# Two heads per group of score matmuls in a differential attention, and split operands over 128 partitions for a sparse attention's scores

## Chip, cores and metric

One core of a Trainium2 chip runs the whole program, one launch. The metric is the device time of that core in microseconds (us), the median of several executions; a profile of one execution goes with it.

## What is computed

Two blocks on 256 tokens of width 1024, all in float32. The first has two layers; each normalises, projects, and merges three branches (a differential attention, a Hyena convolution, a gMLP). The second has a sparse attention and a block attention side by side, a feed-forward part and a gated embedding. The two places of the change, cut to what matters:

```python
def diff_attend(q, k, v, lam):              # 4 heads, each with two halves m of 64 dims
    s = jnp.einsum('bhmqd,bhmkd->bhmqk', qi, k).astype(jnp.float32) * scale
    p = jax.nn.softmax(s, axis=-1)
    w = p[:, :, 0] - lam * p[:, :, 1]
    return jnp.einsum('bhqk,bhkd->bhqd', w.astype(v.dtype), v)

def nsa_mixer(...):                         # 8 query heads, 2 groups g of keys, 64 dims
    ...
    s = jnp.einsum('bgrcd,bgcmd->bgrcm', qc, kg) * ATTN_SCALE     # selected blocks
    ...
    s = jnp.einsum('bgrqd,bgkd->bgrqk', qb, kb) * ATTN_SCALE      # window
    o = g[..., 0:1] * o_c + g[..., 1:2] * o_s + g[..., 2:3] * o_w
```

In layer 0 the first block's attention works on the tokens and on a context of 256 more; in layer 1 only the tokens ask. At 256 tokens the selected and the window branch of the sparse attention both see all earlier keys.

## The kernel before

**Weights and products.** float32 accuracy is kept by splitting operands: a value is written as hi + lo in float32r (hi is a rounded copy, lo the rest), and a product is three matmuls, hi·hi, hi·lo and lo·hi. Weights are streamed: `unit` (L70 to L84) loads 512 KB with a DMA on SP's queue into `raw` (3 buffers), ACT casts it to `hi` (L81), DVE subtracts to `lo` (L82), four buffers each. The projections (`gemm_a`, `gemm_b`, tiles `hTh` and `hTl` of the activations) accumulate in four PSUM banks, `pg`. Everything else shares the other four, `pm`, taken with `bank()`.

**Order.** A scheduler lays out the instructions of each engine before the run, by its own estimates, and mixes attention matmuls among those of the projections. Matmuls issued with `chain` (`mm`, L60 to L63) keep their program order among themselves, but others may be put between. Each engine, SP's DMA queue too, then executes its own list in order and waits where an operand or a buffer is not ready.

**Differential attention** (`diff_tile`, L579 to L630). For a tile of 128 queries, six tiles over the two layers, four heads in turn: two banks of `pm`, one for each half m; six matmuls (three products, two halves), where the halves m = 0 and 1 lie on partitions 0 to 63 and 64 to 127, so each matmul uses 64 rows of the array; maximum (L599), exponential on ACT (L603), the difference of the two softmaxes, transposes into the first bank (L614), their copy `wT` (L616), the product with v into the second (L61 through `mm`), and the copy `ya` (L622) that frees it. That is 6 x 4 x 6 = 144 score matmuls, 512 keys wide in four of the tiles and 256 in two.

**Sparse attention** (`block2`). `qs[t]` of 128 tokens each are normalised and rotated, then transposed by `trans4` and copied by ACT to `q2T` (L245; L1078, L1079), with group g on partitions 64g to 64g + 63. `ck` is copied out of PSUM and `compress` (L958 on) brings it into the tile `cXF` by four DMAs on SP (L964, L965), adds positions on DVE (L970), and runs 16 float32 compress matmuls each for keys and values against `cw` (two records each). The KV projection follows; its keys are transposed (L1105) and copied by ACT into `kv` (`k2T`, L1106). The scores (L1114 to L1117, `soft_pair` L919 to L927) are one float32 matmul of 64 rows for each of the 8 heads and 2 tiles t, 256 columns wide at t = 0 and 512 at t = 1. float32 operands take two passes of the array here, and the trace has two records for each.

```python
            for i, j in ((0, 0), (0, 1), (1, 0)):
                for m in range(2):
                    r = slice(64 * m, 64 * m + 64)
                    self.mm(sb[m][:, :KN], qT[i][r, h, qt * 128:qt * 128 + 128], kT[j][r, h, k0:k0 + KN],
                            i + j == 0, i == 1, i + j + m > 0)
```

`slabs` (L1282) is a pool of ten buffers of 8 KB per partition, used among others for the modulation weights (`ada`).

Of the kernel before, what the change touches and what calls it, by code (L numbers as in the profile page):

```python
# [7 lines left out]
F32 = mybir.dt.float32  # L8
F32R = mybir.dt.float32r
# [22 lines left out]
class Body:  # L32
# [548 lines left out]
    def diff_tile(self, qt, kT, v, keys, qT, nl, y):  # L581
        nc = self.nc
        k0, KN = keys
        nk = KN // 128
        rs = self.col(4, f"rs{qt}")
        so = self.col(4, "so")
        y = y.rearrange("p (h d) -> p h d", h=4)
        for h in range(4):
            sb = [self.bank(), self.bank()]
            mx = self.col(2, "mx")  # L590
            ss = self.col(2, "ssum")
            p = self.att.tile([128, 2, 512], F32, name=self.nm("p"), tag="p")
            for i, j in ((0, 0), (0, 1), (1, 0)):
                for m in range(2):
                    r = slice(64 * m, 64 * m + 64)
                    self.mm(sb[m][:, :KN], qT[i][r, h, qt * 128:qt * 128 + 128], kT[j][r, h, k0:k0 + KN],
                            i + j == 0, i == 1, i + j + m > 0)
            for m in range(2):
                nc.vector.tensor_reduce(mx[:, m:m + 1], sb[m][:, :KN], axis=AX.X, op=OP.max)  # L599
            nb = self.col(2, "nb")  # L600
            nc.vector.tensor_scalar(nb, mx, -0.125, None, op0=OP.mult)
            for m in range(2):
                nc.scalar.activation(p[:, m, :KN], sb[m][:, :KN], AF.Exp, bias=nb[:, m:m + 1], scale=0.125,  # L603
                                     accum_out=ss[:, m:m + 1])
            r1 = self.col(2, "r1")
            nc.vector.reciprocal(r1, ss)
            cf = self.col(1, "cf")
            nc.vector.tensor_scalar(cf, ss[:, 0:1], r1[:, 1:2], nl, op0=OP.mult, op1=OP.mult)
            nc.vector.tensor_copy(rs[:, h:h + 1], r1[:, 0:1])
            w = p[:, 0, :KN]  # L610
            nc.vector.scalar_tensor_tensor(w, p[:, 1, :KN], cf, w, op0=OP.mult, op1=OP.add)
            tp = sb[0].rearrange("p (k t) -> p k t", k=4)
            for k in range(nk):
                nc.tensor.transpose(tp[:, k], w[:, k * 128:k * 128 + 128], self.ident)  # L614
            wT = self.att.tile([128, 4, 128], F32, name=self.nm("wT"), tag="wT")
            nc.scalar.copy(wT[:, :nk], tp[:, :nk])  # L616
            o = sb[1][:, :128]
            for k in range(nk):
                self.mm(o, wT[:, k], v[:, k0 // 128 + k, h * 128:h * 128 + 128], k == 0, k == nk - 1)
            jk = self.att.tile([128, 128], F32, name=self.nm("aj"), tag="aj")  # L620
            nc.scalar.activation(jk, o, AF.Square, accum_out=so[:, h:h + 1])
            nc.vector.tensor_copy(y[:, h], o)  # L622
        nc.vector.tensor_tensor(so, so, rs, op=OP.mult)
        nc.vector.tensor_tensor(so, so, rs, op=OP.mult)
        r = self.col(4, f"ro{qt}")
        nc.vector.tensor_scalar(so, so, 1.0 / 128.0, EPS, op0=OP.mult, op1=OP.add)
        self.rpow(r, so)
        return r, rs
# [287 lines left out]
            nc.vector.tensor_tensor(tm[:, 1, :, o], d[:, :, i], s, op=OP.mult)  # L916
        nc.vector.tensor_tensor(d[:, :, 0:16], tm[:, 0], tm[:, 1], op=OP.add)

    def soft_pair(self, t, units, fold):  # L919
        banks = [self.bank().rearrange("p (m k) -> p m k", m=2) for _ in units]  # L920
        first = True
        for step in zip(*[mms for mms, _, _ in units]):
            for s, (dst, l, r) in zip(banks, step):
                self.mm(s[:, dst, :128 * (t + 1)], l, r, chain=not first)
                first = False
        for s, (_, vs, hs) in zip(banks, units):
            yield hs, *self.soft_unit(t, s, vs, fold, hs)  # L927

# [109 lines left out]
    def block2(self, x, hTp):  # L1038
        nc, a = self.nc, self.a
# [22 lines left out]
        qT, _ = self.pair("q2T")  # L1062
        for jh in range(2):
            nc.sync.dma_start(w1s[0][jh], a["c_w1"][0, jh])
        qs = [self.tf("w") for t in range(2)]
        kv = self.flat("kv2")
        folds = kv[:, 1536:1632].rearrange("p (i a h) -> p i a h", i=4, a=3)
        fold, mfold = [folds[:, t] for t in range(2)], [folds[:, 2 + t] for t in range(2)]
# [6 lines left out]
        for f in range(2):  # L1075
            for i in range(4):
                self.part_a(us[i], 2 * i, f, op, 256, b[:, f * 256:f * 256 + 256], i == 0, i == 3)
        for t in range(2):  # L1078
            self.trans4(qs[t], qT[:, :, t * 128:t * 128 + 128], None)  # L1079
        ck = self.tf("w")  # L1080
        nc.vector.tensor_copy(ck, b)
        gb = self.gbank()
# [5 lines left out]
        for t in range(2):  # L1088
            tp = self.bank()[:, :24]
            nc.tensor.transpose(tp, gT[:, t * 128:t * 128 + 128], self.ident[:24, :24])  # L1090
            g = self.pcv(24)
# [1 line left out]
            gates.append(g)  # L1093
        self.compress(ck.rearrange("p (v t) -> p v t", v=2), kv[:, 1024:1536].rearrange("p (h d) -> p h d", h=8), w1s)
        bs = self.gemm_b(w[W2CH["KV"]], op, [0, 1])
        k2T = kv[:, :512].rearrange("p (s t) -> p s t", s=2)
        v2 = kv[:, 512:1024].rearrange("p (t s d) -> p t s d", t=2, s=2)
        for t in range(2):
            kn = self.tf("w")[:, :256]
            v4 = bs[t].rearrange("p (s v d) -> p s v d", s=2, v=2)  # L1100
            self.norm_rope(kn, v4[:, :, 0], self.gains[:, 2:4], t, 4)
            nc.vector.tensor_copy(v2[:, t], v4[:, :, 1])
            tp = self.bank()[:, :256].rearrange("p (s t) -> p s t", s=2)
            for s in range(2):
                nc.tensor.transpose(tp[:, s], kn[:, s * 128:s * 128 + 128], self.ident)  # L1105
            nc.scalar.copy(k2T[:, :, t * 128:t * 128 + 128], tp)  # L1106
        ynr = self.flat("ynr")[:, :1024].rearrange("p (t d) -> p t d", t=2)
        for t in range(2):
            y = ynr[:, t].rearrange("p (h d) -> p h d", h=8)
            gt = gates[t][:, 8:24].rearrange("p (m h) -> p h m", m=2)  # L1110
            for i in range(4):
                units = []
                for g in range(2):
                    r = slice(64 * g, 64 * g + 64)  # L1114
                    units.append(([(slice(0, 2), qT[r, i, t * 128:t * 128 + 128], k2T[r, :, :128 * (t + 1)])],
                                  lambda m, k, g=g: v2[:, k, m, 64 * g:64 * g + 64], (2 * i + g, 2 * i + g)))
                for (h, _), o, rs in self.soft_pair(t, units, fold[t]):  # L1117
                    cf = self.col(2, "ucf")
                    nc.vector.tensor_tensor(cf, rs, gt[:, h], op=OP.mult)
                    nc.vector.tensor_scalar(y[:, h], o[:, 0], cf[:, 0:1], None, op0=OP.mult)  # L1120
                    nc.vector.scalar_tensor_tensor(y[:, h], o[:, 1], cf[:, 1:2], y[:, h], op0=OP.mult, op1=OP.add)
# [29 lines left out]
        for t in range(2):  # L1151
            c = slice(t * 128, t * 128 + 128)
            self.trans4(ynr[:, t], ynh[:, :, c], ynl[:, :, c])
        ys = self.scr.tile([128, 1024], F32, name=self.nm("ay"), tag="ay", bufs=1).rearrange("p (t d) -> p t d", t=2)
        for t in range(2):
            KN = 128 * (t + 1)
            y = ys[:, t].rearrange("p (h d) -> p h d", h=8)
            for i0 in (0, 2):
                units = []
                for m in range(2):  # L1160
                    r = slice(64 * m, 64 * m + 64)
# [110 lines left out]
    def run(self):  # L1272
# [6 lines left out]
        self.att = P("att", 2)  # L1279
        self.hT = P("hT", 1)  # L1280
        self.wraw, self.whi, self.wlo = P("wraw", 3), P("whi", 4), P("wlo", 4)
        self.slabs = P("slabs", 10)  # L1282
        self.psg, self.psm = P("psg", 4, True), P("psm", 4, True)
        self.ones = self.const.tile([128, 128], F32, name="ones")
        nc.vector.memset(self.ones, 1.0)
# [167 lines left out]
```

## Time and profile before

| | before |
|---|---|
| median of 3 runs | 1395.8 us (1393.54 to 1398.58) |
| profiled execution | 1392.87 us, span 1390.9 |
| TensorE (PE) busy | 1355.7 us, 97% |
| weight loads (PEld) busy | 1134.1 us, 82% |
| VectorE (DVE) / ScalarE (ACT) busy | 64% / 45% |
| chain that ended last | PE 83%, DVE 7%, DMA 4%, ACT 3% |
| read from memory | 203.37 MB, 147 GB/s over the span |

The span is what the profile covers; the device time is some 2 us more. Busy shares are over the whole span. The chain is followed back from the last instruction, at each step to what released it. PE rows of a timeline give the start and the modelled length of matmuls that overlap, so what one costs is read from start to start of neighbours.

### The profile page before, as it was taken

Reading aid. Unit: us, or ns where it says so; the run is one execution under the profiler, and the core shown is the slowest. Engines: PE = TensorE matmul, PEld = TensorE weight load, DVE = VectorE, ACT = ScalarE, POOL = GpSimd, SP = SyncE. Lnnn points to the kernel's source line nnn. Section 1 sums busy time; section 2 is a strip of 40 time slices with the busy share of each in tenths; the row PEclk is TensorE's granted clock in tenths of the full one; section 3 lists DMA queues with packets and bytes.
Section 4 is the critical chain, followed back from the end, with each engine's and each line's share of the span. In section 5 each row is a group of like instructions: output and inputs, shape, how many; then the busy total and the mean of one; then the engine's idle time right before and its main releaser. Section 6 shows DMA issues by size and latency. Waiting matters only on the chain.

```text
span 1390.9 us, 19805 instructions
## 1 busy us (share of the span) xinstructions
PE 1355.7 (97%) x7721; PEld 1134.1 (82%) x7721; DVE 897.1 (64%) x1574; ACT 621.5 (45%) x1046; POOL 43.3 (3%) x55
## 2 busy tenths in 40 slices
PE   6999999999999999999999999999999999999998
PEld 3786888777888888788688899987878897899996
DVE  3757842685388977388856755667776567655545
ACT  3532432564332334375535644554554645444433
POOL 0000000000000000010000000001002000000000
PEclk9999999999999999999999999999999999999999
DMA  9431222112535545327334255558315356665551
GB/s 388 143 107 61 81 89 92 63 46 67 201 111 191 220 178 183 136 92 234 107 96 135 93 171 187 182 165 289 122 57 160 103 173 193 207 204 191 184 182 46
DMA packets 55261, 206.22 MB, mean 148 GB/s; under 512 B 7102, under 2 KB 8320, under 8 KB 51584
## 3 DMA queue, kind: packets, MB, share of 16 engines
q1 hardware_dynamic: 55168, 204.95, 43.6%
q8 instruction: 61, 1.00, 0.3%
q14 instruction: 32, 0.26, 0.1%
HBM read 203.37 MB, written 1.05 MB: 147 GB/s over the span
## 4 chain that ended last, share of the span: by engine, by line
PE 83%; DVE 7%; DMA 4%; ACT 3%; issue 2%; POOL 1%; SPq 0%; POOLq 0%; ACTq 0%; DVEq 0%
PE pg L61 67%; PE pm L61 13%; DVE lo L82 1%; DMA ada<-ada_w 1%; PE pm L243 1%; DMA f<-hy_f_w 1%; DMA raw<-w_in 1%; ACT hi L81 1%; PE pm L614 1%; DMA xs<-x 1%; ACT p L603 1%; PE pm L947 1%; DVE hTl L67 1%; POOL rstd L145 0%; DVE mx L599 0%
## 5 line engine op out<-in xcount | busy, mean ns | idle before, releaser
L82 DVE TENSOR_TENSOR lo<-raw,hi 128x1024 fp32r<-128x1024 f32 (+1 forms) x242 | 293.6, 1215 | 246.2 <-ACT hi L81 245.1
L81 ACT CAST hi<-raw 128x1024 fp32r<-128x1024 f32 (+1 forms) x242 | 252.1, 1044 | 385.4 <-PE pg L61 332.5
L61 PE MATMUL pg<-hTh,hi 128*128 128x256 f32 (+1 forms) x920 | 305.0, 333 | 1.8 <-DMA f<-hy_f_w 1.4
L61 PE MATMUL pg<-hTl,hi 128*128 128x256 f32 (+1 forms) x920 | 305.2, 332 | 1.1 <-DVE hTl L67 1.1
L61 PE MATMUL pg<-hTh,lo 128*128 128x256 f32 (+1 forms) x920 | 303.9, 331 | 0.3 <-DVE lo L82 0.3
L61 PEld LDWEIGHTS pg<-hTh,hi 128*128 128x128 f32 x920 | 174.0, 189 | 24.5 <-issue 4.2
L61 PEld LDWEIGHTS pg<-hTl,hi 128*128 128x128 f32 x920 | 174.2, 189 | 21.0 <-issue 4.3
L61 PEld LDWEIGHTS pg<-hTh,lo 128*128 128x128 f32 x920 | 174.1, 189 | 18.5 <-issue 2.8
L61 PE MATMUL pg<-lo,hTh 128*128 128x512 f32 x400 | 158.7, 397 | 0.5 <-DVE lo L82 0.5
L61 PE MATMUL pg<-hi,hTh 128*128 128x512 f32 x400 | 158.9, 397 | 0.3 <-ACT hTh L66 0.2
L61 PE MATMUL pg<-hi,hTl 128*128 128x512 f32 x400 | 157.5, 394 | 1.0 <-DVE hTl L67 1.0
L82 DVE TENSOR_TENSOR wsl<-raw,wsl 128x1024 fp32r<-128x1024 f32 x66 | 80.2, 1223 | 70.1 <-ACT wsl L81 69.4
L61 PE MATMUL pg<-hTh,wsl 128*128 128x256 f32 x576 | 105.2, 284 | 0.0
L81 ACT CAST wsl<-raw 128x1024 fp32r<-128x1024 f32 x66 | 68.4, 1048 | 80.3 <-PE pg L61 50.3
L61 PEld LDWEIGHTS pg<-hTh,wsl 128*128 128x128 f32 x576 | 90.5, 192 | 0.3
L61 PEld LDWEIGHTS pg<-hi,hTl 128*128 128x128 f32 x400 | 75.2, 188 | 18.1 <-DVE hTl L67 1.9
L61 PEld LDWEIGHTS pg<-lo,hTh 128*128 128x128 f32 x400 | 75.3, 188 | 17.8 <-issue 2.5
L61 PEld LDWEIGHTS pg<-hi,hTh 128*128 128x128 f32 x400 | 75.2, 188 | 17.4 <-issue 1.5
L61 PE MATMUL pg<-hTl,wsl 128*128 128x256 f32 x288 | 81.7, 284 | 0.0
L61 PE MATMUL pg<-gh,lo 128*128 128x512 f32 (+1 forms) x192 | 64.8, 337 | 0.0
L61 PE MATMUL pg<-gh,hi 128*128 128x512 f32 (+1 forms) x192 | 64.7, 337 | 0.0
L61 PE MATMUL pg<-gl,hi 128*128 128x512 f32 (+1 forms) x192 | 64.6, 337 | 0.0
(363 smaller groups left out, 2031.8 us busy)
## 6 DMA issues: line engine op xcount, KB each, us to landing
raw<-w_in SPq DMA_DIRECT2D x172, 512.0 KB, 3.6
raw<-w_ffn_in SPq DMA_DIRECT2D x36, 512.0 KB, 3.6
ada<-ada_wT SPq DMA_DIRECT2D x16, 1024.0 KB, 6.8
raw<-w_branch SPq DMA_DIRECT2D x24, 512.0 KB, 3.5
raw<-w_out SPq DMA_DIRECT2D x24, 512.0 KB, 3.6
raw<-w_ffn_out SPq DMA_DIRECT2D x22, 512.0 KB, 4.0
ada<-ada_w SPq DMA_DIRECT2D x8, 1024.0 KB, 16.3
cw<-c_w SPq DMA_DIRECT2D x4, 1024.0 KB, 8.6
```

The source lines that it names most:

```text
L61: ins = self.nc.tensor.matmul(out, l, r, start=start, stop=stop)
L67: self.nc.vector.tensor_tensor(lo, src, hi.bitcast(F32), op=OP.subtract)
L81: nc.scalar.copy(hi, raw)
L82: nc.vector.tensor_tensor(lo, raw, hi.bitcast(F32), op=OP.subtract)
L243: nc.tensor.transpose(ps[:, k], src[:, k * 128:k * 128 + 128], self.ident)
L603: nc.scalar.activation(p[:, m, :KN], sb[m][:, :KN], AF.Exp, bias=nb[:, m:m + 1], scale=0.125, accum_out=ss[:, m:m + 1])
L614: nc.tensor.transpose(tp[:, k], w[:, k * 128:k * 128 + 128], self.ident)
L947: nc.tensor.transpose(tp[:, m, k], p[:, m, k * 128:k * 128 + 128], self.ident)
```

## The change

Three edits.

1. `diff_tile`: for each even head all four `pm` banks are taken, and the score matmuls of this head and the next are issued as one chain of twelve, in each product head 1 before head 0 and m = 1 before m = 0. All that follows for a head is as before.
2. `block2`: the queries `qT` are split into hi and lo (a tile `q2s`), and four DMAs for each t, from SBUF to SBUF on SP's queue, bring them to `sq`: hi on partitions 0 to 63 and lo on 64 to 127, for each group g. The keys are split out of PSUM (`k2s`, instead of the copy on ACT), and eight DMAs for each t bring them to `sk`: `a_` = 0 holds hi on both halves of the partitions, `a_` = 1 holds lo on both. A score is then two float32r matmuls over all 128 partitions, accumulated: (q hi, q lo) against hi, and against lo. `soft_pair` accumulates a unit's matmuls with `acc`.
3. `slabs` has 12 buffers; the memory comes from a smaller scratch for dynamic DMAs.

```diff
         for h in range(4):
-            sb = [self.bank(), self.bank()]
+            if h % 2 == 0:
+                sbs = [[self.bank(), self.bank()] for _ in range(2)]
+                go = False
+                for i, j in ((0, 0), (0, 1), (1, 0)):
+                    for hh in (1, 0):
+                        for m in (1, 0):
+                            r = slice(64 * m, 64 * m + 64)
+                            self.mm(sbs[hh][m][:, :KN], qT[i][r, h + hh, qt * 128:qt * 128 + 128],
+                                    kT[j][r, h + hh, k0:k0 + KN], i + j == 0, i == 1, go)
+                            go = True
+            sb = sbs[h % 2]
...
-            for i, j in ((0, 0), (0, 1), (1, 0)):
-                for m in range(2):
-                    r = slice(64 * m, 64 * m + 64)
-                    self.mm(sb[m][:, :KN], qT[i][r, h, qt * 128:qt * 128 + 128], kT[j][r, h, k0:k0 + KN],
-                            i + j == 0, i == 1, i + j + m > 0)
...
-    def soft_pair(self, t, units, fold):
+    def soft_pair(self, t, units, fold, acc=False):
...
+        if acc:
+            for s, (mms, _, _) in zip(banks, units):
+                for i, (dst, l, r) in enumerate(mms):
+                    self.mm(s[:, dst, :128 * (t + 1)], l, r, i == 0, i == len(mms) - 1)
...
+        sq = self.flat("sq", F32R).rearrange("p (g i t) -> p g i t", g=2, i=4)
+        sk = self.flat("sk", F32R).rearrange("p (a g s t) -> p a g s t", a=2, g=2, s=2)
         for t in range(2):
-            self.trans4(qs[t], qT[:, :, t * 128:t * 128 + 128], None)
+            c = slice(t * 128, t * 128 + 128)
+            self.trans4(qs[t], qT[:, :, c], None)
+            hl = self.att.tile([128, 2, 4, 128], F32R, name=self.nm("q2s"), tag="p")
+            self.split(hl[:, 0], hl[:, 1], qT[:, :, c])
+            for g in range(2):
+                for j in range(2):
+                    nc.sync.dma_start(sq[64 * j:64 * j + 64, g, :, c].bitcast(F32), hl[64 * g:64 * g + 64, j].bitcast(F32))
...
-            nc.scalar.copy(k2T[:, :, t * 128:t * 128 + 128], tp)
+            hl = self.att.tile([128, 2, 2, 128], F32R, name=self.nm("k2s"), tag="p")
+            self.split(hl[:, 0], hl[:, 1], tp)
+            for g in range(2):
+                for j in range(2):
+                    for a_ in range(2):
+                        nc.sync.dma_start(sk[64 * j:64 * j + 64, a_, g, :, t * 128:t * 128 + 128].bitcast(F32),
+                                          hl[64 * g:64 * g + 64, a_].bitcast(F32))
...
-                    r = slice(64 * g, 64 * g + 64)
-                    units.append(([(slice(0, 2), qT[r, i, t * 128:t * 128 + 128], k2T[r, :, :128 * (t + 1)])],
+                    q = sq[:, g, i, t * 128:t * 128 + 128]
+                    units.append(([(slice(0, 2), q, sk[:, a_, g, :, :128 * (t + 1)]) for a_ in range(2)],
...
-        self.slabs = P("slabs", 10)
+        self.slabs = P("slabs", 12)
...
-    nc = bacc.Bacc("TRN2", target_bir_lowering=False, num_devices=1)
+    nc = bacc.Bacc("TRN2", target_bir_lowering=False, num_devices=1, dynamic_dma_scratch_size=128)
```

The scheduler lays out the new program, so the order of instructions moves as well. TensorE at the second pair of heads of the first tile in layer 0 (`pm` a bank, `kT_255` and `kT_256` hi and lo of the keys, `pg` a projection), before:

```order
L61 MATMUL pm_351_1902<-kT_255_1358,qT_300_1657 128x512
L61 MATMUL pg_504_2403<-hTl0_178,hi_511_2437 128x512
L61 MATMUL pg_504_2403<-hTh0_177,lo_512_2438 128x512
L61 MATMUL pm_352_1903<-kT_255_1358,qT_300_1657 128x512
L61 MATMUL pm_342_1867<-v_257_1360,wT_349_1893 128x128 x4
L61 MATMUL pm_351_1902<-kT_256_1359,qT_300_1657 128x512
L61 MATMUL pm_352_1903<-kT_256_1359,qT_300_1657 128x512
L61 MATMUL pm_351_1902<-kT_255_1358,qT_301_1658 128x512
L61 MATMUL pm_352_1903<-kT_255_1358,qT_301_1658 128x512
```

And now:

```order
L61 MATMUL pm_354_1905<-kT_255_1358,qT_300_1657 128x512
L61 MATMUL pg_506_2405<-hTl0_178,hi_511_2437 128x512
L61 MATMUL pg_506_2405<-hTh0_177,lo_512_2438 128x512
L61 MATMUL pm_353_1904<-kT_255_1358,qT_300_1657 128x512
L61 MATMUL pm_334_1833<-v_257_1360,wT_349_1893 128x128 x4
L61 MATMUL pm_352_1903<-kT_255_1358,qT_300_1657 128x512
L61 MATMUL pg_506_2405<-hTh0_177,hi_511_2437 128x512
L61 MATMUL pg_506_2405<-hTl0_178,hi_511_2437 128x512
L61 MATMUL pg_506_2405<-hTh0_177,lo_512_2438 128x512
L61 MATMUL pm_351_1902<-kT_255_1358,qT_300_1657 128x512
L61 MATMUL pm_354_1905<-kT_256_1359,qT_300_1657 128x512
```

Before, the first matmul of each of the two banks stood apart and ten followed in one piece (six of this head's, less two, and the next head's six). Now the first matmuls of three banks stand apart, and the rest, nine, follow from the fourth on.

SP's queue at the compress stage (`sq`, `cXF` and weight loads `raw`), before:

```order
L80 DMA raw_1587_8536<-w_in_2 128x1024 [waits DMAHW1_49,DVE_49]
L964 DMA cXF_1563_8411<-w_1558_8376 64x2x256 [waits DVE_49]
L965 DMA cXF_1563_8411<-w_1558_8376 64x2x240
L964 DMA cXF_1563_8411<-w_1558_8376 64x2x256
L965 DMA cXF_1563_8411<-w_1558_8376 64x2x240 [waits DMAHW2_49]
L80 DMA raw_1590_8554<-w_in_2 128x1024 [waits DMAHW3_49,Activation_49]
```

And now, behind the four copies of the first half (t = 0):

```order
L1097 DMA sq_1556_8364<-q2s_1561_8385 64x4x128 [waits DMAHW2_49,Activation_49]
L1097 DMA sq_1556_8364<-q2s_1561_8385 64x4x128 [waits DMAHW3_49,DVE_49]
L1097 DMA sq_1556_8364<-q2s_1561_8385 64x4x128 [waits DMAHW4_49]
L1097 DMA sq_1556_8364<-q2s_1561_8385 64x4x128 [waits DMAHW5_49]
L974 DMA cXF_1567_8427<-w_1562_8392 64x2x256 [waits DMAHW6_49,PE_49]
L975 DMA cXF_1567_8427<-w_1562_8392 64x2x240 [waits DMAHW7_49]
L974 DMA cXF_1567_8427<-w_1562_8392 64x2x256 [waits DMAHW0_49]
L975 DMA cXF_1567_8427<-w_1562_8392 64x2x240 [waits DMAHW1_49]
L80 DMA raw_1591_8552<-w_in_2 128x1024 [waits DMAHW2_49]
L80 DMA raw_1594_8570<-w_in_2 128x1024 [waits DMAHW3_49]
```

All eight query copies stand ahead of the cXF copies, the second four waiting for the second half's cast on ACT and subtraction on DVE, and a weight load that stood ahead of cXF now stands behind it.

## Rows read from the trace of the kernel before

**Rows 1.** The page: busy time per engine; TensorE's granted clock in forty slices, in tenths.

```profile
PE 1355.7 (97%) x7721; PEld 1134.1 (82%) x7721; DVE 897.1 (64%) x1574; ACT 621.5 (45%) x1046; POOL 43.3 (3%) x55
...
PEclk9999999999999999999999999999999999999999
```

**Rows 2.** Timeline of PE, first 24 us: start, us, instructions, [idle before <-releaser].

```profile
15.34 0.69 PE L735 MATMUL pm<-packA,xs 128*128 128x128 f32 x2 [2.00 <-DVE xs L723]
```

**Rows 3.** Timeline of PE in the differential attention of layer 0.

```profile
263.23 0.50 PE L61 MATMUL pm<-kT,qT 64*128 64x512 f32 x1
263.66 0.50 PE L61 MATMUL pg<-hTl,hi 128*128 128x512 f32 x1
263.99 0.40 PE L61 MATMUL pg<-hTh,lo 128*128 128x512 f32 x1
...
265.83 1.81 PE L61 MATMUL pm<-kT,qT 64*128 64x512 f32 x10
267.57 0.50 PE L61 MATMUL pg<-hTh,hi 128*128 128x512 f32 x1
```

**Rows 4.** Tile qT: its score matmuls, and idle time before them (us, times).

```profile
L61 PE MATMUL pm<-kT,qT x144: 271/393/502, 253.0 to 791.1; 64*128 64x512 f32 x96, 64*128 64x256 f32 x48
...
  DVE ya L622: 2.5, 8
```

**Rows 5.** Timeline of PE at the sparse scores, t = 0 and t = 1.

```profile
991.21 1.67 PE L61 MATMUL pm<-kv,q2T 64*128 64x256 f32 x8
992.81 0.39 PE L61 MATMUL pg<-hTl,hi 128*128 128x256 f32 x1
993.03 0.28 PE L61 MATMUL pg<-hTh,lo 128*128 128x256 f32 x1
993.15 0.28 PE L61 MATMUL pg<-hTh,hi 128*128 128x256 f32 x1
...
997.84 0.70 PE L61 MATMUL pm<-kv,q2T 64*128 64x256 f32 x2
998.47 0.44 PE L947 MATMUL pm<-packA,p 128*128 128x128 f32 x2
...
1013.54 2.95 PE L61 MATMUL pm<-kv,q2T 64*128 64x512 f32 x8
1016.42 0.39 PE L61 MATMUL pg<-hTl,hi 128*128 128x256 f32 x1
...
1022.64 0.28 PE L61 MATMUL pg<-hTl,hi 128*128 128x256 f32 x1
1022.85 1.12 PE L61 MATMUL pm<-kv,q2T 64*128 64x512 f32 x2
1023.91 1.10 PE L61 MATMUL pm<-kv,wT 128*128 128x64 f32 x8
```

**Rows 6.** Timeline of SP's queue at the compress stage; and its DMAs, us to landing.

```profile
964.61 0.68 SPq L964 DMA_DIRECT2D cXF<-w  x1
965.34 1.07 SPq L965 DMA_DIRECT2D cXF<-w  x1
...
cXF<-w SPq DMA_DIRECT2D x2, 128.0 KB, 3.4
```

**Rows 7.** Timelines of ACT and DVE at the compress stage.

```profile
964.81 1.05 ACT L81 CAST hi<-raw 128x1024 fp32r<-128x1024 f32 x1
...
965.89 1.23 DVE L82 TENSOR_TENSOR lo<-raw,hi 128x1024 fp32r<-128x1024 f32 x1 [1.31 <-ACT hi L81]
```

**Rows 8.** Timeline of PE at the compress stage.

```profile
970.62 0.39 PE L61 MATMUL pg<-lo,hTh 128*128 128x512 f32 x1
970.85 0.39 PE L61 MATMUL pg<-hi,hTl 128*128 128x512 f32 x1
971.75 1.93 PE L61 MATMUL pm<-cw,cXF 128*32 128x256 f32 x32 [0.52 <-issue]
```

**Rows 9.** Timeline of ACT at the copy of the transposed keys.

```profile
990.45 0.37 ACT L1106 COPY kv<-pm 128x256 f32<-128x256 f32 x1 [0.70 <-PE pm L1105]
```

More of the change, by code (lines that the diff above doesn't have):

```diff
@@ L917, in norm_rope @@
         nc.vector.tensor_tensor(d[:, :, 0:16], tm[:, 0], tm[:, 1], op=OP.add)
-    def soft_pair(self, t, units, fold):
+    def soft_pair(self, t, units, fold, acc=False):
         banks = [self.bank().rearrange("p (m k) -> p m k", m=2) for _ in units]
[L921 to L925, printed above, removed]
+        if acc:
+            for s, (mms, _, _) in zip(banks, units):
+                for i, (dst, l, r) in enumerate(mms):
+                    self.mm(s[:, dst, :128 * (t + 1)], l, r, i == 0, i == len(mms) - 1)
+        else:
+            first = True
+            for step in zip(*[mms for mms, _, _ in units]):
+                for s, (dst, l, r) in zip(banks, step):
+                    self.mm(s[:, dst, :128 * (t + 1)], l, r, chain=not first)
+                    first = False
         for s, (_, vs, hs) in zip(banks, units):
@@ L1095, in block2 @@
         bs = self.gemm_b(w[W2CH["KV"]], op, [0, 1])
-        k2T = kv[:, :512].rearrange("p (s t) -> p s t", s=2)
         v2 = kv[:, 512:1024].rearrange("p (t s d) -> p t s d", t=2, s=2)
@@ L1113, in block2 @@
                 for g in range(2):
-                    r = slice(64 * g, 64 * g + 64)
-                    units.append(([(slice(0, 2), qT[r, i, t * 128:t * 128 + 128], k2T[r, :, :128 * (t + 1)])],
+                    q = sq[:, g, i, t * 128:t * 128 + 128]
+                    units.append(([(slice(0, 2), q, sk[:, a_, g, :, :128 * (t + 1)]) for a_ in range(2)],
                                   lambda m, k, g=g: v2[:, k, m, 64 * g:64 * g + 64], (2 * i + g, 2 * i + g)))
-                for (h, _), o, rs in self.soft_pair(t, units, fold[t]):
+                for (h, _), o, rs in self.soft_pair(t, units, fold[t], True):
                     cf = self.col(2, "ucf")
```

## The prediction

> **What bounds the kernel now.** I read the page first. TensorE is busy for 1355.7 of 1390.9 us (97%), and the granted clock stands at full speed in all forty slices [rows 1]. So what counts is TensorE time taken out or put in, and any stretch in which TensorE waits. The longest row of idle time ahead of a TensorE instruction in the stretches I read is 2.00 us, near the start [rows 2]. That is the scale for a new gap.
>
> The timeline of TensorE in the differential attention comes next. Its score matmuls use 64 of the 128 array rows, and the first one of a run costs far more than the next ones. One alone, 512 wide, holds TensorE from 263.23 to 263.66, 0.43 us; the full-array matmul behind it takes 0.33 (263.66 to 263.99); ten in a row take 265.83 to 267.57, 1.74 us [rows 3]. Each further one of a run costs (1.74 − 0.43)/9 = 0.146 us, less than a full 128-row matmul of that width, which takes 0.23 [rows 8]: the two halves m run side by side. What is paid per **run** is the start: 0.43 − 0.15 = 0.28 us, 0.10 more on the matmul behind it (0.33 against 0.23), and about as much on the one ahead of it (0.21 in 1022.64 to 1022.85, where 0.12 is the pace: 993.03 to 993.15) [rows 3, 5, 8]. Together 0.48 us for every further run that the same 144 matmuls are cut into.
>
> The timeline of the sparse attention shows the same switch, and fp32 operands: each instruction leaves two records (x8 for four, x2 for one). Four of them take 1.60 us at t = 0 (991.21 to 992.81) and 2.88 at t = 1 (1013.54 to 1016.42); one alone takes 0.63 (997.84 to 998.47) and 1.06 (1022.85 to 1023.91) [rows 5].
>
> **The change, part by part.** The sum is made against the profiled execution, 1392.9 us (span 1390.9 and 2 around it). The median of the three runs is 1395.8, 2.9 above; I add the difference at the end.
>
> *Differential attention.* Nothing is removed: 144 score matmuls before and after. The edit asks for twelve in one chain for two heads, which would make 12 runs. The order does not give that: the first four of a chain each start a fresh bank, the four banks come free one by one, and other matmuls are put between. The typical chain is 1, 1, 1 and 9. Counted over all of it, 31 runs become 39. Eight more runs at 0.48 make **+3.8 us**. Some of the 2.5 us in which instructions here stood idle behind the copy that frees a bank [rows 4] should go, as the singles now start with the first bank instead of waiting for a later one; I take 1.0 off: **+2.8**. Bounds: +1.3 when all 2.5 go; +6.3 when each added run meets one more such wait, 2.5/8 = 0.31 us. I price all eight as 512 wide, although 48 of the 144 are 256 wide [rows 4], so I am on the dear side there.
>
> *Sparse scores.* Out: 16 fp32 instructions in 10 runs. t = 0: 1.60 + 4 × 0.63 = 4.1; t = 1: 2.88 + 4 × 1.06 = 7.1; ten switches at 0.2 (both neighbours) = 2.0; together 13.2 us [rows 5]. In: 32 full-array matmuls of split operands, 16 of 256 columns at 0.12 and 16 of 512 at 0.23 [rows 5, 8], 5.6 us, with no switch. **−7.6 us**; bounds −6.6 (only the matmul behind pays the switch) and −8.4 (the waits inside the old runs go as well). The two accumulated matmuls carry all four products, so nothing else is added on TensorE.
>
> *What feeds them.* Added: two q2s splits and two k2s splits (a cast on ACT, a subtraction on DVE, the k2 copy on ACT drops out), and 24 DMAs on SP's queue. ACT and DVE time is hidden by itself (64% and 45% busy [rows 1]); what is not hidden is the queue. SP issues in order, and the eight q2 copies now stand ahead of the four cXF copies and of two weight loads. One issue of a small copy takes 0.68 us, in one place 1.07 [rows 6].
>
> The compress matmuls wait for cXF: first cXF issue 964.61, first compress matmul 971.75, 7.1 us later [rows 6, 8]. In the new order the second half's q2s cast comes behind a weight cast that ends at 964.81 + 1.05 = 965.9, so at 966.5 (0.6 us, as it has half the elements of the 1.05); its subtraction comes behind one that ends at 965.89 + 1.23 = 967.1, so at 967.85 [rows 7]. The hi copy of group 0 goes out at 966.5, its lo copy at 967.85, two more at 0.65 each, and the first cXF copy at 969.8. That is 5.2 us later, and compress starts at 977.0. TensorE has no more to do in between: its last KV matmul of the loaded units starts at 970.85 [rows 8]. The new order puts three KV matmuls ahead of compress that stood behind it, 3 × 0.23 = 0.7 us. So **+4.5 us** of idle time; bounds +3.0 (issues at half the price) and +6.5 (issues at 1.07 and the weight cast later). The two weight loads behind cXF go out at 972.4 and should land some 3.5 us later (a cXF copy takes 3.4 [rows 6]); their cast and subtraction, 1.05 and 1.23 [rows 7], end at 978.2, before compress does (977.0 + 1.9 [rows 8]), so I cost their lateness at nothing: compress covers it. If compress started on time this would be late next, by up to 2 us.
>
> Then sk: before, the scores stood right behind the transposes of k2 (991.21). The new order puts 21 matmuls of 0.12 between, 2.5 us. The split's hi half is there at 990.45 + 0.37 = 990.8 [rows 9], and eight copies for t = 0 take until 990.8 + 8 × 0.65 = 996.0 to issue. With 3 us to landing (3.4 for a cXF copy [rows 6]) the four pieces are there at about 994.5, 995.8, 997.2 and 998.5, while TensorE comes for them at 993.4 and then with 0.6 to 0.9 us of other work between. Wait by wait this is 1.1 + 0.2 + 0.4 + 0.2, of which I take **+1.5**; bounds 0.5 and 5 (issues at 1.07). What is queued behind on SP is one more weight load, delayed by some 5 us, for a projection that has two loaded units ahead of it: hidden.
>
> *Slabs 10 to 12, scratch smaller.* Two modulation loads of layer 0 go out earlier, past other loads on SP; the weights that they pass are needed some hundreds of us later. Nothing, either way.
>
> Sum: 2.8 − 7.6 + 4.5 + 1.5 = **+1.2 us**: 1394.1 for the profiled execution, 1397.0 on the median. About 0.3%, 4.2 us, is what a measurement of this kernel can tell from no change; so the forecast is no measurable change.
>
> **The rivals.**
> *The clock falls in the compress gap.* Some 5.7 us without a TensorE instruction is nearly three times the longest idle time seen (2.00 us, at full clock) [rows 1, 2]. No row of before shows a lower clock, so the price is an estimate: at 1.2 GHz instead of 2.4 a matmul of 512 columns takes 0.46 instead of 0.23, and were it so for the rest of the KV projection (24 matmuls), it adds 5.4: 1.2 + 5.4 = +6.6, 1402.4. It decides once the gap is long enough for the granted clock to fall at all, and the trace does not show where that is. The Trainium skill, "TensorE: Matmul & The Clock Gate", section "HAM oscillation — how this bites in real kernels", says that a TensorE left idle between bursts is set back to its lower clock; by that rule this gap would bring the fall, and the time would be this rival's 1402.4. The trace of before agrees as far as it goes: it has no such gap, and no fall. I give it 0.17.
>
> *SP's issues cost 1.07, not 0.65.* In the gap four issues stand between the lo half and the last cXF copy, +1.7; on sk eight, +3.4: together +6.3, 1402.1. For it: 965.34 with 1.07, a copy of the same kind. Against: its neighbour, 0.68 [rows 6]. 0.13.
>
> *The gap is shorter and the sk pieces hidden.* If SP issues these copies in half the time, the gap is 3.0 and sk 0.5; with the attention at its low end (+1.3) and the scores at −8.4 the sum is −3.6, 1392.2, and with the gap covered by any TensorE work that comes free, a little below. 0.20 for a gain beyond 0.3%, since all four must lean one way.
>
> *The group is not a group.* If the twelve matmuls ran unbroken, 12 runs in place of 31 would save 19 × 0.48 = 9 us. The order excludes it; it stands in my sum as eight more runs, and gets no chance of its own.
>
> **How the numbers follow.** My forecast of no measurable change has 0.50, faster 0.20, slower 0.30 (the two rivals above). Predicted 1397.0. Low end 1391, where the third rival lies; high end 1404, above both slow rivals and with the attention term a little above what I take. Outside I leave some 0.2: the slow rivals together, and a fall in both.
>
> **What would show it.** Right: in the timeline some 39 runs of 64-row score matmuls, singles at 0.43 us; sparse scores at 0.12 and 0.23 each with no double records; compress matmuls 5 us behind the last KV matmul with the cXF copies as releaser; short waits for sk pieces. Wrong: a compress gap below 2 us (then faster), rows of KV matmuls at twice their length behind the gap (clock), waits of several us ahead of the sparse scores, or score runs of 12 unbroken.

## The result: 0.6% slower, and the profile after

The changed kernel takes 1406.3 us in the median of five executions (1401.7 to 1410.5), the kernel before 1394.7 in five beside them: 1.0062 of before, 95% interval 1.0035 to 1.0089. A later set of nine executions beside 26 of before gave 1.0067 (1.0040 to 1.0094). By these ratios it is slower by about 9 us; the medians lie 11.6 and, in the later set, 7.9 us apart. The forecast of no measurable change was wrong, and 1406.3 lies above its high end of 1404; "slower" had 0.30.

The profiled execution took 1406.28 us. Its page, the span, the busy times and the chain:

```profile
span 1404.4 us, 19824 instructions
...
PE 1359.4 (97%) x7721; PEld 1137.1 (81%) x7721; DVE 900.2 (64%) x1578; ACT 621.8 (44%) x1048; POOL 41.0 (3%) x55
...
PEclk9999999999999999999999999999999999999999
...
PE 78%; DVE 9%; DMA 5%; ACT 3%; issue 2%; POOL 1%; SPq 1%; POOLq 0%; ACTq 0%; DVEq 0%
```

TensorE is 3.7 us busier than before [rows 1], but the span grew by 13.5, so most of it is waiting. To see where, I take the same projection matmul in both timelines at the ends of each stage and compare how far it has moved. In the table "changed, 2nd" is the later trace of the same kernel, "before, 2nd" one of before; the others are the runs below. Each entry is what a stage adds against the first trace of before, in us; "whole" goes up to the last projection matmul.

| trace | attention, layer 0 | filter loads, layer 1 | attention, layer 1 | sparse and block attention | all else | whole |
|---|---|---|---|---|---|---|
| changed | +4.6 | +3.9 | +0.6 | +2.7 | +1.8 | +13.4 |
| changed, 2nd | +4.7 | +0.2 | +0.6 | +9.8 | +4.3 | +19.4 |
| before, 2nd | 0.0 | −0.1 | 0.0 | +0.8 | −1.0 | −0.3 |
| grouping alone | +4.6 | −0.2 | +5.1 | +4.5 | +3.1 | +17.2 |
| grouping, forward order | +3.0 | +5.4 | +0.7 | +6.1 | +0.9 | +16.0 |
| slabs alone | 0.0 | +3.4 | −0.4 | +1.8 | −1.4 | +3.4 |
| sparse scores alone | 0.0 | +0.1 | −0.4 | +5.2 | +1.0 | +6.0 |
| same, q2 copies late | 0.0 | −0.2 | −0.4 | −0.2 | +0.7 | −0.1 |
| same, 8 k2 copies | 0.0 | +2.6 | −0.4 | +0.7 | +3.6 | +6.5 |
| same, late, 16 from ACT | 0.0 | −0.4 | −0.4 | +3.8 | +1.0 | +4.1 |
| same, late and 8 | 0.0 | −0.6 | −0.4 | −5.6 | −0.3 | −6.9 |
| grouping, late and 8 | +4.7 | +0.2 | +0.5 | −5.5 | −0.8 | −0.9 |

The column of layer 0 repeats to 0.2 us wherever the code is the same. The filter column does not, though no kernel's code differs there, and the two traces of the changed kernel stand 3.7 apart: it is chance. The sparse column holds both. It ends at a matmul that runs at 1082 us in before, and in eight of the thirteen traces, the second of before among them, that lies in a stretch at the lower clock in the block attention. Taken 2 us later it would be +1.7 for "before, 2nd" and +0.5 for "q2 copies late"; ahead of the block attention (1075.14 in before) it is +4.1 for the sparse scores alone, −1.2 with the q2 copies late, −1.0 with 8 k2 copies and −4.0 with both.

The clock row of the page shows the same 9 in all forty slices as before's [rows 1], although this execution's granted clock fell three times between 653 and 1145 us. A slice is 35 us long here and a 9 stands for 90% or more, so such a row does not show a short fall.

**The compress gap.** The forecast gap is there. TensorE around it, and SP's queue:

```profile
981.25 0.39 PE L61 MATMUL pg<-hi,hTl 128*128 128x512 f32 x1
984.72 3.44 PE L61 MATMUL pm<-cw,cXF 128*32 128x256 f32 x32 [3.08 <-issue]
988.08 0.50 PE L61 MATMUL pg<-hi,hTh 128*128 128x512 f32 x1
```

```profile
970.82 8.49 SPq L1097 DMA_DIRECT2D sq<-q2s  x8
979.41 0.59 SPq L974 DMA_DIRECT2D cXF<-w  x1
...
981.65 0.59 SPq L975 DMA_DIRECT2D cXF<-w  x1
982.28 17.01 SPq L80 DMA_DIRECT2D raw<-w_in  x9
1008.01 11.48 SPq L1128 DMA_DIRECT2D sk<-k2s  x16
```

The last KV matmul starts at 981.25, compress at 984.72, 3.08 us idle, where before had 0.52 [rows 8]. The first cXF copy goes out at 979.41. With the 9.3 to 9.7 us that the matmuls ahead of the stage have moved by then, that is 969.7 to 970.1 on the time scale of before; the forecast said 969.8. The first compress row then takes 3.36 us to the next matmul (984.72 to 988.08) against 1.87 before (971.75 to 973.62): the granted clock is at its lower level there.

**The start of layer 1.** The first filter matmul waits for a small load. After, and below it before:

```profile
648.18 0.28 PE L61 MATMUL pg<-hTh,lo 128*128 128x256 f32 x1
651.55 0.61 PE L61 MATMUL pm<-f 33*64 33x256 f32 x2 [3.09 <-DMA f<-hy_f_w]
...
653.39 0.63 PE L61 MATMUL pg<-hi,hTl 128*128 128x512 f32 x1
653.81 0.63 PE L61 MATMUL pg<-hi,hTh 128*128 128x512 f32 x1
654.24 0.63 PE L61 MATMUL pg<-lo,hTh 128*128 128x512 f32 x1
...
656.77 0.40 PE L61 MATMUL pg<-lo,hTh 128*128 128x512 f32 x1
657.00 0.40 PE L61 MATMUL pg<-hi,hTl 128*128 128x512 f32 x1
```

```profile
643.20 0.28 PE L61 MATMUL pg<-hTh,lo 128*128 128x256 f32 x1
644.35 0.61 PE L61 MATMUL pm<-f 33*64 33x256 f32 x2 [0.87 <-DMA f<-hy_f_w]
```

The same load lets TensorE start 3.37 us behind the last projection matmul, instead of 1.15. Then the matmuls of 512 columns, which take 0.23 [rows 8], stand 0.42 to 0.43 apart from 653.39 on and 0.23 apart again from 656.77: 1.2 GHz between stretches at 2.4. Nothing in the change touches this place.

**The attention.** Two stages by windows, after and then before (columns: window, length, busy time of PE, PEld, DVE, ACT and POOL, granted clock, DMA share, GB/s):

```profile
243.00:366.00 123.00, 120.15 (x602) 90.44 (x602) 75.99 (x190) 57.20 (x146) 4.04 (x4) 1.00 0.20 64
757.00:823.00 66.00, 65.07 (x498) 58.56 (x497) 51.67 (x108) 37.69 (x81) 2.03 (x2) 1.00 0.36 113
```

```profile
242.50:361.00 118.50, 117.47 (x602) 90.30 (x602) 75.11 (x190) 57.29 (x146) 4.04 (x4) 1.00 0.20 66
748.50:814.00 65.50, 65.03 (x498) 58.26 (x498) 51.04 (x108) 38.09 (x81) 2.03 (x2) 1.00 0.35 113
```

In layer 0 TensorE's idle time grows from 1.0 us to 2.9 (123.00 − 120.15), its busy time by 2.7, for seven further runs (21 become 28 there). The waits are of this kind, with the singles of a chain between them:

```profile
317.28 0.41 PE L619 MATMUL pm<-packA,p 128*128 128x128 f32 x2 [0.83 <-DVE r L611]
...
319.07 0.38 PE L61 MATMUL pm<-kT,qT 64*128 64x256 f32 x1
...
320.95 0.38 PE L61 MATMUL pm<-kT,qT 64*128 64x256 f32 x1
...
337.33 0.41 PE L619 MATMUL pm<-packA,p 128*128 128x128 f32 x2 [0.54 <-DVE r L611]
```

**The sparse scores.** Two records per score, none of them double:

```profile
1022.36 0.48 PE L61 MATMUL pm<-sk,sq 128*128 128x256 f32 x2
1022.67 0.28 PE L61 MATMUL pg<-hTh,lo 128*128 128x256 f32 x1
...
1046.11 0.71 PE L61 MATMUL pm<-sk,sq 128*128 128x512 f32 x2
1046.66 0.40 PE L61 MATMUL pg<-lo,hTh 128*128 128x512 f32 x1
```

A pair 256 wide takes 0.31 us (1022.36 to 1022.67), one 512 wide 0.55 (1046.11 to 1046.66), so 0.155 and 0.275 each, not 0.12 and 0.23.

### The profile page after: what moved, and what is told of

It reads as the page before. It is cut to its first block, busy times and chain, and to the rows that moved or that the text cites. A ratio compares the mean times of both kernels' runs of the same rounds, so it can differ in the third digit from the quotient of the medians.

```text
span 1404.4 us, 19824 instructions
## 1 busy us (share of the span) xinstructions
PE 1359.4 (97%) x7721; PEld 1137.1 (81%) x7721; DVE 900.2 (64%) x1578; ACT 621.8 (44%) x1048; POOL 41.0 (3%) x55
## 4 chain that ended last, share of the span: by engine, by line
PE 78%; DVE 9%; DMA 5%; ACT 3%; issue 2%; POOL 1%; SPq 1%; POOLq 0%; ACTq 0%; DVEq 0%
PE pg L61 62%; PE pm L61 13%; DVE lo L82 2%; DMA ada<-ada_w 1%; DMA f<-hy_f_w 1%; PE pm L243 1%; ACT hi L81 1%; ACT p L608 1%; DMA raw<-w_in 1%; DVE mx L604 1%; PE pm L619 1%; DMA xs<-x 1%; DVE hTl L67 1%; DMA raw<-w_ffn_in 1%; DVE wsl L82 1%
```

## The experiments

All ratios are to the kernel before, run on the same chip beside it. The runs come in three sets on three chips, so that runs are compared by their ratios.

### The parts, each alone

Only the grouping (the `diff_tile` of the change, all else as before):

> Only the differential attention's grouping by two heads; sparse scores and slabs as before. Theory 1 (the three parts add up, and this one costs what its stage shows in the changed kernel's trace, 4.6 us in layer 0 and 0.5 in layer 1): about +5 us, the filter loads at the start of layer 1 land as before (first filter matmul some 1.1 us behind the last projection matmul), and no row at half clock there. Rival (a mere shift in time lengthens the wait at the start of layer 1 and brings stretches at half clock with it): +7 to +10 us, with the wait of some 3 us and a slow stretch behind it. Second rival (the grouping costs nothing by itself): within 1.5 us of before.

1406.2 us in the median of six, 1.0078 (1.0050 to 1.0106), 11 us, twice what the first theory said. Layer 0 costs what it costs in the change, and the filter loads came in time in its trace, so they don't belong to it. Layer 1 costs 5.1 instead of 0.6: with ten slabs the scheduler gives another order there, 42 runs in all instead of 39, and one score matmul waits 1.57 us for a bank (at 804.96), with a stretch at the lower clock behind it. Its compress waits 1.99 us for cXF too, though its code there is that of before. Of the time, then, part is this kernel's own order and part chance.

Only the sparse scores, with the slabs they need (`diff_tile` as before):

> Only the sparse scores with split operands (and the 12 slabs and smaller scratch that they need); differential attention as before. Theory 1: the stage gives +2.6 us as in the changed kernel's trace (scores 4.2 less, compress gap 2.9 more, compress at half clock 1.5 more, waits around the scores the rest), so about +2.5 with a slow stretch at compress, about +1 without. Rival (the start of layer 1 belongs to slabs or scratch): +2.2 to +3.8 more, so +5 to +6.5.

1398.6, 1.0029 (1.0012 to 1.0046), 4 us slower. The 3.06 us gap at compress is there again, with the lower clock behind it. This part was to gain 1.6.

Only the slabs and the scratch:

```diff
-        self.slabs = P("slabs", 10)
+        self.slabs = P("slabs", 12)
...
+ dynamic_dma_scratch_size=128
```

> Only 12 slabs and the smaller scratch. Theory 1: nothing, within 1 us of before, the start of layer 1 as before. Rival (the early modulation loads or the smaller scratch make the filter loads at the start of layer 1 land 2.2 us later): +2.2 to +4 us, with the filter matmul waiting some 3 us there.

1394.7, 0.9995 (0.9979 to 1.0012): nothing. Its trace did show the late filter loads (+3.4 in the table), but so did one without these slabs (+5.4), and six traces of kernels that have them did not. The rival falls.

### SP's order at cXF

The sparse scores alone, with the q2 copies issued behind the cXF copies:

```diff
-            for g in range(2):
-                for j in range(2):
-                    nc.sync.dma_start(sq[64 * j:64 * j + 64, g, :, c].bitcast(F32), hl[64 * g:64 * g + 64, j].bitcast(F32))
+            hls.append((c, hl))
...
     def compress(self, ck, vbig, w1s, copies):
...
             nc.sync.dma_start(X[64:128, :, g, 0:240], ck[64 * g:64 * g + 64, :, 16:256])
+        copies()
```

> As the run with the sparse scores alone, but the eight q2 copies stand on SP's queue behind the four cXF copies instead of ahead of them. Theory 1 (the compress gap comes from SP's order): the first cXF copy goes out some 5 us earlier than there, TensorE idles under 1 us ahead of compress, no slow stretch at compress, and the time is 3 to 4.5 us below that run, so 1 to 2 us below before. Rival (the gap comes from the splits on ACT and DVE, or from landing times): the gap stays above 2 us and the time within 1 us of that run. Second rival (the q2 copies are then late for the scores): gap gone, but waits of 2 us or more ahead of the first sparse scores.

1393.2, 0.9991 (0.9974 to 1.0008): 5 us below the sparse scores alone, at the time of before. Its timeline, and SP's queue at the keys:

```profile
970.39 0.39 PE L61 MATMUL pg<-hi,hTl 128*128 128x512 f32 x1
971.07 1.93 PE L61 MATMUL pm<-cw,cXF 128*32 128x256 f32 x32 [0.29 <-issue]
...
1014.34 0.39 PE L61 MATMUL pg<-hTh,lo 128*128 128x256 f32 x1 [0.74 <-DVE lo L82]
```

```profile
991.60 11.29 SPq L1128 DMA_DIRECT2D sk<-k2s  x16
1002.93 29.05 SPq L80 DMA_DIRECT2D raw<-w_in  x9
```

The gap is 0.29 us: the order on SP made it. But the stage then stands at −0.2, not at −4 or so, because the queue has a second place. The sixteen k2 copies take SP 11.29 us; the weight loads behind them start at 1002.93, and at 1014.34 TensorE waits 0.74 us for a weight's lo, with the lower clock from 1015.0 on. The run with half the k2 copies, below, has this wait no more. A part of the −0.2 is the block attention's slow stretch.

### The number of k2 copies

The sk tile laid out so that hi and lo of a group lie side by side, and one copy takes both: eight instead of sixteen.

```diff
-                    for a_ in range(2):
-                        nc.sync.dma_start(sk[64 * j:64 * j + 64, a_, g, :, t * 128:t * 128 + 128].bitcast(F32),
-                                          hl[64 * g:64 * g + 64, a_].bitcast(F32))
+                    nc.sync.dma_start(sk[64 * j:64 * j + 64, g, :, :, t * 128:t * 128 + 128].rearrange("p a s t -> p (a s) t").bitcast(F32),
+                                      hl[64 * g:64 * g + 64].rearrange("p a s t -> p (a s) t").bitcast(F32))
```

With the q2 copies late as well:

> As the run with the q2 copies behind cXF, but the sixteen k2 copies become eight of twice the size (hi and lo in one). Theory (SP's issue time of 11 us for the k2 copies delays the weight loads behind them and the scores): SP is done some 5 us earlier, the waits of 0.3 us ahead of the first sparse scores and of about 1 us for a weight behind them go, 1 to 2 us below that run, so 2 to 4 us below before. Rival (those waits come from the softmax): within 1 us of that run.

1388.4, **0.9957 (0.9943 to 0.9972)**: 6 us faster than before, the fastest kernel here, and 2 us more than the theory's upper end. Its rows:

```profile
969.96 0.39 PE L61 MATMUL pg<-hi,hTl 128*128 128x512 f32 x1
970.90 1.93 PE L61 MATMUL pm<-cw,cXF 128*32 128x256 f32 x32 [0.56 <-issue]
...
997.96 0.47 PE L61 MATMUL pm<-sk,sq 128*128 128x256 f32 x2 [0.42 <-DMA sk<-k2s]
```

```profile
992.46 5.73 SPq L1127 DMA_DIRECT2D sk<-k2s  x8
998.23 31.13 SPq L80 DMA_DIRECT2D raw<-w_in  x9
```

SP is free at 998.23, 5.7 us after it began; one wait of 0.42 us for a k2 copy is left. The stage gives −5.6 us. Of these, −4.0 stands ahead of the block attention, close to the 4.2 that the new scores save by their starts (below). The other 1.6 comes at a wait that is not the scores'. Ahead of the block attention's first score matmuls TensorE waits for ACT's copy mT, first in before, then here:

```profile
1078.38 1.20 PE L61 MATMUL pm<-mT 64*128 64x128 f32 x8 [1.09 <-ACT mT L245]
```

```profile
1072.66 0.71 PE L61 MATMUL pm<-mT 64*128 64x128 f32 x8
```

Eleven traces have this wait, 1.09 to 1.64 us; only the two with late q2 copies and eight k2 copies do not. In these the weight cast that stands ahead of the copy on ACT starts 4.0 us before these matmuls, elsewhere 2.6. No expectation had this: the program was laid out anew, and its order came out so. What that order is worth by itself was not run.

The eight k2 copies alone, the q2 copies ahead of cXF as in the change:

> The sparse scores alone with eight k2 copies instead of sixteen, but the q2 copies ahead of cXF as in the change. Theory (two separate costs on SP's queue: the order at cXF, some 4 us by the first pair of runs, and the number of k2 copies, some 5 us by the second): 4 us above the run with both mended, about 1 to 2 us below before, with the gap of 3 us at compress and a slow stretch behind it. Rival (only the two together pay, or the k2 copies were the whole of it): within 1.5 us of the run with both mended, or at the time of the sparse scores alone.

1397.3, 1.0003 (0.9986 to 1.0019): about 6 us above the run with both, and 4 below the sparse scores alone. Both places cost, each by itself: late q2 copies are worth 5.3 us with sixteen k2 copies and 6.4 with eight, halving the k2 copies 3.6 us with the q2 copies ahead of cXF and 4.7 behind them.

The sixteen k2 copies issued by ACT, the q2 copies late on SP:

```diff
-                        nc.sync.dma_start(sk[
+                        nc.scalar.dma_start(sk[
```

> As the run with the q2 copies behind cXF, but the sixteen k2 copies are issued by ACT instead of SP. Theory (SP's issue time matters, ACT has room): 1 to 2 us below that run. Rival (each issue holds ACT for 0.6 us, 10 us in all, and the casts and exponentials of the stage wait behind it): 1 to 4 us above that run, with idle time of TensorE ahead of weights' hi or of p.

1397.6, 1.0023 (1.0009 to 1.0036): 4 us worse than from SP. ACT's timeline, and TensorE at the first scores:

```profile
992.02 5.45 ACTq L1128 DMA_DIRECT2D sk<-k2s  x8
997.57 0.37 ACT L66 CAST k2s<-pm 128x256 fp32r<-128x256 f32 x1 [5.58 <-DMA sk<-k2s]
...
998.83 5.67 ACTq L1128 DMA_DIRECT2D sk<-k2s  x8
1004.61 0.46 ACT L947 ACTIVATE p<-pm,nb,kv 128x128 f32<-128x128 f32 x1 [5.73 <-DMA sk<-k2s]
```

```profile
997.10 0.36 PE L61 MATMUL pm<-sk,sq 128*128 128x256 f32 x1 [2.31 <-DMA sk<-k2s]
...
999.86 0.77 PE L61 MATMUL pm<-sk,sq 128*128 128x256 f32 x2 [1.46 <-DMA sk<-k2s]
```

Eight issues hold ACT for 5.5 us; the second half's cast waits behind them until 997.57, a weight's cast after it, and the exponential of the first scores until 1004.61. The rival's time came, but not by its waits alone: TensorE's idle time is ahead of the first scores, 2.31 and 1.46 us, for the copies themselves, which took 3.4 us in the median to land (2.0 from SP), and the granted clock is 0.50 from 999.0 to 1005.8.

### The order of heads in a chain

The grouping alone, with head 0 and m = 0 first:

```diff
-                    for hh in (1, 0):
-                        for m in (1, 0):
+                    for hh in (0, 1):
+                        for m in (0, 1):
```

> Only the differential attention's grouping, as in the first run, but with head 0 ahead of head 1 and m = 0 ahead of m = 1 in each product; still 39 runs of score matmuls by the order, 8 more than before. Theory A (most of the cost is the runs: eight or more further starts at 0.48 us, and the matmuls around them): about the first run's time, +5 to +9 us on before. Rival B (most is waiting for the first head's softmax, which the reversed order makes late): 2 us or more below the first run, with the idle time ahead of the transposes (four places of 0.6 to 1.0 us in layer 0 there) mostly gone.

1398.5, 1.0030 (1.0011 to 1.0049): 4 us above before, 7 below the reversed order, with 39 runs. In layer 0 it gives +3.0 instead of +4.6. Both theories hold in part: the first head's softmax comes late where head 1 goes first (the waits ahead of the transposes in layer 0 sum to 1.6 us here and to 2.6 there, so they shrink and do not go), and some 3.7 us (3.0 + 0.7) stay with the forward order, against 3.8 forecast for the eight runs. Most of the rest of the 7 is layer 1, where this order of instructions has no wait for a bank. Its trace is its slowest execution: both places that depend on landings were late in it (+5.4 and +6.1).

### Second traces, and the mended change

The kernel before, once more:

> The kernel before, once more, for a second trace. Theory (the waits for the filter loads at the start of layer 1 and for cXF at compress differ from run to run of the same program, since their landing depends on other transfers): the idle time at one of the two places differs by over 0.5 us from the first trace (0.9 and 0.5 us there), and stretches at half clock appear where that trace has none. Rival (the program repeats itself, and such waits belong to the edits): both places within 0.2 us of the first trace, full clock throughout.

1392.6 in its one execution. At the two places 0.73 and 0.89 us of idle time (0.87 and 0.52 in the first trace), so the theory's half microsecond was not met by this pair; but its block attention has a stretch at the lower clock (from 1081.0 on), where the first trace has none before the last few microseconds. The program is the same, so a fall there needs no edit.

The changed kernel, once more:

> The changed kernel once more, for a second trace and a narrower interval. Theory (the late filter loads at the start of layer 1 are chance, the compress gap is not): the gap of 3 us at compress is there again, the wait for the filter loads may be 0.9 to 3.5 us; the time 1.005 to 1.009 of before, that is 7 to 12 us. Rival (the first five runs were unlucky): 1.003 or less.

1404.8, 1.0067, as before. The filter loads were in time (+0.2), the gap was there, and a longer one at sk:

```profile
977.84 0.39 PE L61 MATMUL pg<-hi,hTl 128*128 128x512 f32 x1
981.29 2.75 PE L61 MATMUL pm<-cw,cXF 128*32 128x256 f32 x32 [3.06 <-issue]
...
1012.93 0.78 PE L61 MATMUL pm<-sk,sq 128*128 128x256 f32 x2 [1.90 <-DMA sk<-k2s]
1013.51 0.42 PE L61 MATMUL pg<-hTh,lo 128*128 128x256 f32 x1
1013.73 0.41 PE L61 MATMUL pg<-hTh,hi 128*128 128x256 f32 x1
```

Compress starts 3.06 us idle again. At 1012.93 TensorE waits 1.90 us for a copy of k2, and the 256-wide matmuls behind it go 0.22 apart instead of 0.12.

The change with both mends of SP's queue:

> The changed kernel with both mends of SP's queue (q2 copies behind cXF, eight k2 copies), the differential attention grouped as in the change. Theory (parts add: the run with both mends is 6 us below before, the grouping by two heads costs 7 to 11): 1 to 5 us above before. Rival (the grouping costs only where SP's queue is already late): 2 us or more below before.

1395.0, 0.9982 (0.9964 to 1.0000), 2.5 us below before by the ratio. The theory said 1 to 5 us above, so it is missed, and the time is the rival's. The rival's reason does not hold either: with SP's queue mended, layer 0 still costs 4.7 us in its trace. Against the mended sparse scores alone (0.9957) the grouping costs 3.5 us here; against the sparse scores as changed (1.0029) it cost 4.6 to 5.3. So of the change's 9 us the grouping is about half.

## Why the prediction was wrong

- **What bounds the kernel** held. TensorE is the bound; every loss that was found is TensorE's time or its waiting.
- **Attention, +2.8**: the sign was right, 5.1 was measured (4.6 and 0.6 in the table), inside the bounds of 1.3 and 6.3. The 31 runs did become 39. The part that failed is the 1.0 us taken off for waits. The 2.5 us [rows 4] were idle time of the weight loads (PEld), which overlap PE; TensorE itself stood idle for only 1.0 us in all of layer 0. They did fall, to 0.7, but new waits for the softmax came in their place (0.83 us at 317.28, 0.54 at 337.33), and TensorE's idle time grew by 1.8 us in layer 0. That the chain puts head 1 first was in the diff and I gave it no price; turned round, it gives back 1.6 us there. The start of a run was priced well enough: 2.7 us of busy time for seven runs in layer 0 is 0.38 each, 0.48 was forecast.
- **Scores, −7.6**: too large, by 3.4 us, the largest miss in size. By rows 5 they cost 11.2 us without the switches; the new ones take 7.0 by their starts, −4.2. I priced each at the pace of projection matmuls; issued in pairs between others, they took 0.155 and 0.275 us. With SP's queue mended the stage gives −4.0 up to the block attention, switches and new waits included, so the 2.0 us for switches did not come on top.
- **Compress gap, +4.5**: the first cXF copy came when forecast, within 0.3 us. The gap cost 2.6 us of idle time (3.08 against 0.52), less than the low bound of 3.0, since I carried over the 7.1 us from first copy to compress; it was 5.3 (979.41 to 984.72). The copies landed in 2.4 us here and in 3.4 before, where DVE also had a weight's subtraction ahead. With the lower clock that follows, the order at cXF is worth 5.3 to 6.4 us in time.
- **sk, +1.5, and the weight load behind it "hidden"**: this is the step whose mechanism failed. The copies themselves were waited for little in one trace (0.6 us, by weight loads) and 1.90 us in the other. But eight copies fewer are worth 3.6 to 4.7 us (1.0029 to 1.0003, 0.9991 to 0.9957), and with them go waits for a weight and the lower clock that follows one of them. The queue's other users were not hidden.
- **The clock rival**, 0.17, is nearest to what came, and I left it out of the sum: the gap brought the lower level in all four traces of kernels that have it. Its price at compress is 1.5 us by the rows, not 5.4, since the matmuls behind compress are back at full pace; and it comes back at other places. The Trainium skill's rule ("TensorE: Matmul & The Clock Gate", "HAM oscillation — how this bites in real kernels"), that idle time between bursts sets the clock back, agrees with this trace, where the fall came with the idle 3.08 us.
- **The SP rival** is refuted: sixteen copies in 11.48 us are 0.72 each, not 1.07. The number of issues mattered.
- **Slabs: nothing** was right.

The sum by what was measured: attention 5.1, gap 2.6, scores −4.2. The lower clock adds some 2.5 us, its 1.5 at compress included: the mean granted clock is 0.9945 over the changed kernel's fourteen executions and 0.9963 over 84 of before, which is 7.7 and 5.2 us of lost time, by my estimate. That makes 6.0. In the first trace, waits of over 0.15 us between compress and the block attention (for p, a weight's lo and others) add 2.1 us more than in before. The 9 us of the result are so accounted for to within its interval, 5 to 12 us; how far each of these last waits belongs to the k2 copies was not measured.

## What to carry to other kernels

Count what a new copy does to the queue it stands in, and who is behind it: here 24 small copies on SP cost more than the matmuls they fed had saved, and moving eight of them and halving the others turned 4 us of loss into 6 of gain, with the same arithmetic; some 1.6 of that gain came from a new order further on, which no expectation had. A group that needs all banks at once is not a group when they come free one by one; read the scheduled order. And where TensorE is dense, price a gap with the lower clock that may follow it.

## What the runs showed of the hardware

- Behind the first 40 us, TensorE stood idle for 3.00 to 3.38 us seven times, in five of thirteen traces; each time matmuls at half the pace began within 2 us of its end. Of six idle times of 1.90 to 2.67 us, five were followed so. The wait for mT ahead of the block attention's scores, 1.09 to 1.64 us in eleven traces, was followed by the lower clock within 3.2 us in eight of them; the two traces without it have no fall there. The 1.11 us ahead of its up projection (tile ym), in every trace, were followed so in three of the thirteen. So a wait of over 1 us may cost the clock or not, and one execution does not tell.
- The same program does not repeat itself. 84 executions of the kernel before, beside the runs above, ran from 1390.0 to 1405.1 us, at granted clocks from 1.00 to 0.99, 0.996 in the mean. The trace that the prediction was made on had full clock nearly throughout and stood 2.9 us below the median; a part of such a difference is this. The mended kernel, with fewer gaps, runs at 0.998.
- The landing of the same small loads differs from trace to trace. The forward grouping has the code of before at both places, and its trace has these rows (the filter matmul and then compress):

```profile
649.91 1.08 PE L61 MATMUL pm<-f 33*64 33x256 f32 x2 [3.38 <-DMA f<-hy_f_w]
```

```profile
979.83 0.39 PE L61 MATMUL pg<-hi,hTl 128*128 128x512 f32 x1
983.22 2.25 PE L61 MATMUL pm<-cw,cXF 128*32 128x256 f32 x24 [3.00 <-issue]
```

The second hyena weight, 16 KB, took 4.1 to 7.2 us from issue to landing over the traces, cXF's copy 2.4 to 6.2. I had taken such a wait for a property of the code. What makes a landing late was not tested.
